# A column schedule, the rows of two weights and the first gate frames moved in a one-core encoder layer

## The chip, the core and the metric

The kernel runs on one core of one Trainium2 chip. The metric is device time in microseconds, of one launch; lower is better. All data are float32, and every product must keep almost all of that precision.

## What is computed

One layer over 2048 frames of a new stream and 32 frames of a running one, width 1024. Two mixers share one input projection; then come an output projection, a gate and an embedding product.

```python
hn = rmsnorm(h, g_mix)
proj = hn @ w_in                       # (2080, 1024) @ (1024, 3072)
hA, bA, cA, zA, vB, zB = split(proj)   # 512 columns each
u = cA * hA                            # causal width-3 convolution over frames
yA = bA * conv3(u) * silu(zA)
pooled = trailing_mean(vB, windows=(2, 4, 8, 16)) - vB
yB = (pooled @ pool_w per group) * pool_scale * silu(zB)
h = h + concat([yA, yB]) @ w_out       # 1024 x 1024
gate = sigmoid(rmsnorm(h, g_ple) @ w_ple_gate)
h = h + (p @ w_ple) * gate             # p has 256 columns
y = rmsnorm(h, g_final)
```

The last rows of u and vB are returned as states.

## The kernel before

**Products.** Each float32 operand is split by a cast on ScalarE into a rounded high part and by a subtraction on VectorE into the rest (`split`, L81 and L84; weights L197 and L198); three matmuls per block then take high x high, high x low, low x high. On top of this, two-by-two blocks of frames and weights are multiplied by a scheme of seven products in place of eight. A frame group thus needs seven pieces named 11, 21, T2, T1, T3, 22 and T4 (sums and differences of its quarters), a weight the pieces 11, 12, S2, S1, S3, S4 and 22. In the w_out and gate products frames and weights have changed sides: there the weights have the pieces T1 to T4.

**Stage 1, input projections (0 to 572 us).** Frames go in two groups of 1024 (`GROUPS`). A unit (group, j) computes 128 columns of each of the six projections, in three pairs: zb/v, c/h and za/b, in this order. Twelve matmuls of 128 x 512 per step, seven steps per pair, named x, y and z by their PSUM banks (x_zbv, y_zbv, z_zbv ...). Raw weight columns are loaded by SP as raw_zbv_0a, raw_zbv_0b and so on (L550; half a megabyte, from rows of w_in). While group 0 is computed, the pieces of group 1 are prepared: `next_columns` takes the four 128-frame columns of both halves of the group, one after the other (the fourth first, then 0, 1, 2). For a column, `frame_sums` loads two frame tiles (xt), takes their sums of squares on ScalarE (L94, kept in program order), normalizes them on VectorE (L453), transposes on TensorE (pt_g, L460, kept in program order too), forms the seven pieces and stores each on POOL's queue to DRAM (L523, p_d11, p_dT1 ...). It is a generator; `at_pace(steps, num, den)` advances it by num/den steps at every step of a unit, 24 calls per unit and 72 in the three units (0,1) to (0,3):

```python
for i, _ in enumerate(frame_sums(ahead.pop(c), f"g1_{c}", dst)):
    if i == 10 and after is not None:
        ahead[after] = columns_in(1, after, nc.gpsimd)
    yield
yield
```

So the loads of the next column's frame tiles are issued at the eleventh step, on POOL. When group 0 is done, `load_group` reads the seven pieces back in one 2 MB DMA each, on POOL (L537, tiles B). The first unit of group 1 runs its zb/v and c/h pairs in turn, and loads raw_ch into the ring `xin` (four buffers), which the staged pieces and frame tiles of the columns use too (`spare_ring`).

**Stage 2, output projection (572 to 757 us).** First the embedding products of seven frame tiles (e, L109; p @ w_ple, with pps the prepared frames of p and wp the weight), then w_out for pairs of tiles (`seven`, x_o, y_o, z_o, L185). Meanwhile the pieces of w_out are made from its upper rows wo_t 0 to 3 (`tops`) and lower rows wo_b 0 to 3 (`bots`) by `weight_parts` (L195 to L198). Frames y and residual rows x come in by SP; tiles lie in the rings xh (4 buffers), ya (5), cmb (8), qa (2) and st (4).

**Stage 3, gate (758 to 978 us).** The other nine embedding products (e_7 to e_14 and the short e_16) run with pps loads from pp_d and the weight wq from wl_d. wg_t and wg_b are the rows of the gate weight. Then follow the gate's seven products per pair of tiles (x_g, y_g, z_g). A pair's frames are made by `prep_g(i)`, two steps: `turned_here` (the odd tile, hn_1, four loads and a transpose on VectorE, L1486) and a second step with `turned` (the even tile: copies ho on ScalarE L1473, transposes pth on TensorE L1475) and the sums and splits.

The scheduler orders instructions on each engine by the program's order, the dependences and its own estimate of times; loads are issued by SP in one order, and by POOL in another, and each queue's next instruction waits for the one ahead.

Of the kernel before, what the change touches and what calls it, by code (L numbers as in the profile page):

```python
# [36 lines left out]
def trunk(ctx, tc, x_p, x_s, c_conv, c_pool, p_p, p_s, g_mix, w_in, conv_w, conv_b, pool_w,  # L37
# [320 lines left out]
    def ring4(t, name):  # L358
        return t.tile([P, D], F32, tag="t", name=name)

    def load_y(i, m, pool=None):
        a = []
        for half in range(2):
            t = ring4(pool or ya, f"y_{i}_{half}").rearrange("p (k t) -> p k t", k=KH)
            nc.sync.dma_start(t[:, :, :m], y_d[half * KH:half * KH + KH, :, i * P:i * P + m].rearrange("k p t -> p k t"))
            a.append(t)
        return a
# [7 lines left out]
    with ExitStack() as s1:  # L375
# [98 lines left out]
        def frame_sums(xs, tag, dst):  # L474

            xs = [x_stat(x, True) for x in xs]
            yield  # L480
            for x in xs:
                normal(x)
                yield
            yield
            f12, f1, f21 = (ftile(f"{c}_{tag}") for c in ("f12", "f1", "f21"))
            sub = lambda o, x, y: nc.vector.tensor_tensor(o, x, y, op=ALU.subtract)
            steps = four(xs, tag)
            p11, p12 = next(steps)
            nc.scalar.copy(f12, p12)
            sub(f1, f12, p11)  # L490
            dst("11", p11)
            yield
            dst("T1", f1)
            yield
            p21, p22 = next(steps)
            nc.scalar.copy(f21, p21)
            sub(f1, p22, f1)
            sub(f12, p22, f12)
            yield
            dst("21", p21)  # L500
            yield
            dst("22", p22)
            yield
            dst("T2", f1)
            sub(f21, f21, f1)
            yield
            dst("T3", f12)
            yield
            dst("T4", f21)
            yield  # L510
# [736 lines left out]
        for gi, tbs in enumerate(GROUPS):  # L1247
            if gi == 1:
                B = load_group(1)
            for j in range(4):  # L1250
                u = Unit(gi, tbs, j)
                if gi + j == 0:
                    u.plain()
                    B0["T4"] = piece_of(seventh("B0_T4"), 0)
                    nc.sync.dma_start(B0["T4"].bitcast(F32), p_d["T4"])
                    p_d["T4"] = tc.dram_tile([P, KH, 2, NB], F32, name="p_dT4b")
                    aside = at_pace(next_columns(3, 0, 1, 2), 3, 4)
                    continue
                if gi == 1 and j == 1:
                    aside = at_pace(chain(turn_p(), new_frames(), ple_weights()), 1, 1)  # L1260
                u.seven(B, aside, gi == 1 and j == 0)
# [3 lines left out]
    with ExitStack() as s2:  # L1265
# [88 lines left out]
        S, W = {}, {}  # L1354
        with tc.issue_after(last_raw):
            early_pps = [load_pps(qa.tile([P, 2, 2, P], F32R, tag="q", name=f"pps_{i}"), i, nc.sync) for i in range(2)]
            first_y = load_y(0, 2 * P, xh)
            tops, _ = rows_of_weight(ya, "wo_t", w_out, 0)
        weight_slot(W, "wo", *PLACES[0])
        near = weight_seventh(W, "wo")  # L1360
        for i in range(2, EARLY):
# [7 lines left out]
            loaded.append(last.ins)  # L1369

        more = prep_h(0, lower_rows)
        first_x = [load_rows(xh, "x", b, x_p) for b in range(2)]
        weight_parts(W, tops, None, "11", "T1")
        weight_slot(W, "wo", *PLACES[1])
        space = acts[0].tile([P, SLOT], F32, tag="hn", name="eouts")
# [67 lines left out]
        weight_parts(W, tops, None, "11", "T1")  # L1443
        shared = slot("wq")
        wp = [[shared[:, (2 * k + h) * D:(2 * k + h + 1) * D] for h in range(2)] for k in range(2)]
        for k in range(2):
            for h in range(2):
                nc.sync.dma_start(wp[k][h].bitcast(F32), wl_d[k][h])
        bots, _ = rows_of_weight(cmb, "wg_b", g_d, 1)

        rest_e = [*range(EARLY, NT - 2), NT - 1]

        def ring(what, i):
            if what == "pps":
                return st.tile([P, 2, 2, P], F32R, tag="t", name=f"pps_{i}")
            if what == "out" and rest_e.index(i) % 4 < 2:
                return cmb.tile([P, D], F32, tag="c", name=f"eout_{i}")
            return ring4(xh, f"e{what}_{i}")

        _, run = embed(rest_e, wp, ring, nc.gpsimd)  # L1460
        for c in range(len(rest_e)):
            run(c)


        def turned(i):

            r, n = tiles[i]
            t = load_rows(ya if i else xh, "hn", i, h_d, queue=nc.sync).rearrange("p (q k c) -> p k q c", q=4, k=KC)
            out = []
            for half in range(2):  # L1470
                pt = tbank(f"pth_{i}_{half}")
                o = qa.tile([P, KH, P], F32, tag="q", name=f"ho_{i}_{half}")
                nc.scalar.copy(o[:n].rearrange("p k (q c) -> p k q c", q=4), t[:n, half * KH:half * KH + KH])  # L1473
                for k in range(KH):
                    nc.tensor.transpose(pt[:, k * P:k * P + n], o[:n, k], ident[:n, :n])  # L1475
                out.append(pt.rearrange("p (k t) -> p k t", k=KH))
            return out
# [178 lines left out]
        def prep_g(i):  # L1656
# [18 lines left out]
            def second():  # L1675
                a21, a22 = lower
                s1 = comb("S1", a21, a22, ALU.add, whole)
                a11, a12 = turned(i)
                put("11", a11)
                s2 = comb("S2", s1, a11, ALU.subtract)  # L1680
                s3 = comb("S3", whole(a11), a21, ALU.subtract, whole)
                put("12", a12)
                put("S2", s2)
                s4 = comb("S4", a12, s2, ALU.subtract)
                put("S1", s1)
                put("S3", s3)
                put("S4", s4)
                put("22", a22, whole)
# [3 lines left out]

        S = {}
        steps = prep_g(0)
        steps[2]()
        weight_slot(W, "wg", *PLACES[1])
        weight_parts(W, tops, bots, *PLACES[1])
        W["21"] = halves(shared)[2:]
# [5 lines left out]
        W["T4"] = halves(shared)[:2]  # L1704
        for k in range(KH):
            weight_part(W, "T4", k, tops[k], bots[k], True)
        steps[3]()

        def short_gate():
            n = tiles[NT - 1][1]  # L1710
            A = short("gl", turned(NT - 1), n)
            h, e = (load_rows(*a) for a in ((xh, "h", NT - 1, h_d), (ya, "e", NT - 1, e_d)))
            yield
            plain("gl", A, W, n, *short_ops(h, e, n))
            done_g(NT - 1, h)
            yield

        short_steps = short_gate()
        for i in range(0, NT - 3, 2):
            A = S.pop(i)  # L1720
            h = [load_rows(xh, "h", i + b, h_d) for b in range(2)]
            e = [load_rows(ya, "e", i + b, e_d) for b in range(2)]
            seven(f"g{i}", A, W, *gate_ops(h, e, P, f"g{i}", i), prep_g(i + 2))
            done_g(i, h[0])
            if i in (2, 4):
                next(short_steps)
            if i + 2 < NT - 3:
                done_g(i + 1, h[1])
# [29 lines left out]
```

## Time and profile before

| | |
|---|---|
| three runs | 979.29, 979.32, 973.89 us; median 979.29 |
| profiled execution | 979.49 us |
| its span, first to last instruction | 977.7 us |
| TensorE matmul busy | 909.3 us, 93% of the span |
| VectorE busy | 697.0 us, 71% |
| ScalarE busy | 458.4 us, 47% |
| GpSimd (POOL) busy | 148.5 us, 15% |
| mean granted TensorE clock | 0.973 of full speed |

Engines are called PE (TensorE), PEld (its weight loads), DVE (VectorE), ACT (ScalarE), POOL and SP. In a row, `out<-in` are tiles by their names, without buffer numbers; `x12` is a count; what stands in brackets at a row's end is the idle time before it and what ended this. SPq is an instruction that issues a DMA on SP's queue. The profile's views cut the same execution in different ways: groups of instructions, waits, the chain of waits from the end back, the timeline of an engine, windows with the busy time of each engine, and the DMA view.

### The profile page before, as it was taken

How to read it: one execution, taken by the hardware profiler on the slowest of the kernel's cores; microseconds unless marked ns; L12 is line 12 of the kernel's file. 1: busy time of each engine (PE TensorE's matmuls, PEld its weight loads, DVE VectorE, ACT ScalarE, POOL GpSimd, SP SyncE). 2: the span in 40 equal slices, each digit the busy share in tenths (PEclk: the TensorE clock that was granted, in tenths of full speed). 3: DMA queues.
4: the chain of work that ended last, by engine and by line, in shares of the span. 5: the costliest groups of instructions: out<-in, count | busy, mean ns of one | idle time of the engine just before them, and what ended most of it. 6: DMA issues, size and time to landing. Idle time of an engine off the chain costs nothing.

```text
span 977.7 us, 12213 instructions
## 1 busy us (share of the span) xinstructions
PE 909.3 (93%) x4186; PEld 727.9 (74%) x4186; DVE 697.0 (71%) x1148; ACT 458.4 (47%) x828; POOL 148.5 (15%) x289
## 2 busy tenths in 40 slices
PE   8999999998950999999999998999999889999996
PEld 6788877887840888866678886778788668777885
DVE  6994888896920678763776759956565859689884
ACT  7643544554500444442344347444344656455553
POOL 3110031221220103110000010121211201111112
PEclk9999999999985999999999999999999899999999
DMA  8265294565599217487764285885677784546553
GB/s 267 59 194 199 82 288 151 188 209 165 170 382 375 65 46 238 144 297 239 219 196 134 94 309 220 257 255 200 214 268 255 251 294 150 191 155 238 181 194 132
DMA packets 115099, 199.57 MB, mean 204 GB/s; under 512 B 13270, under 2 KB 72062, under 8 KB 114013
## 3 DMA queue, kind: packets, MB, share of 16 engines
q1 hardware_dynamic: 93469, 127.67, 40.6%
q0 software_dynamic: 19120, 66.72, 20.0%
q10 hardware_dynamic: 2448, 4.39, 1.2%
q8 instruction: 33, 0.54, 0.2%
q14 instruction: 29, 0.24, 0.1%
HBM read 133.06 MB, written 65.67 MB: 203 GB/s over the span
## 4 chain that ended last, share of the span: by engine, by line
PE 51%; DMA 12%; DVE 8%; issue 6%; ACT 3%; POOL 1%; SPq 0%; POOLq 0%; ACTq 0%; DVEq 0%
PE x_o L185 6%; PE x_zbv L616 5%; PE x_ch L616 5%; PE x_g L185 5%; DMA raw_ch_0a<-in_w_in_dram 5%; PE x_zab L616 4%; PE z_ch L616 3%; PE z_g L185 3%; PE e L109 3%; PE z_o L185 3%; PE z_zbv L616 3%; PE z_zab L616 2%; PE y_o L185 1%; PE new L1112 1%; DMA hn<-h_d 1%
## 5 line engine op out<-in xcount | busy, mean ns | idle before, releaser
L616 PE MATMUL x_ch<-B,w_ch 128*128 128x512 f32 x84 | 22.0, 414 | 34.7 <-ACT w_ch L81 34.7
L185 PE MATMUL x_o<-wo_T,y_S 128*128 128x512 f32 x192 | 46.6, 392 | 4.0 <-ACT c_o L1285 3.4
L185 PE MATMUL z_g<-wg,g_S 128*128 128x512 f32 x192 | 47.9, 394 | 0.1
L185 PE MATMUL z_o<-wo,y_S 128*128 128x512 f32 x192 | 47.6, 390 | 0.0
L185 PE MATMUL x_g<-wg_T,g_S 128*128 128x512 f32 x192 | 46.6, 390 | 0.0
L616 PEld LDWEIGHTS x_ch<-B,w_ch 128*128 128x128 f32 x84 | 16.7, 201 | 39.2 <-ACT w_ch L81 35.1
L185 PEld LDWEIGHTS x_o<-wo_T,y_S 128*128 128x128 f32 x192 | 35.8, 188 | 12.7 <-ACT c_o L1285 4.3
L616 PE MATMUL x_zbv<-B,w_zbv_S 128*128 128x512 f32 x168 | 42.5, 403 | 3.0 <-ACT zs L936 3.0
L616 PE MATMUL x_zab<-B,w_zab_S 128*128 128x512 f32 x168 | 41.1, 393 | 0.9 <-ACT V L936 0.9
L616 PE MATMUL x_ch<-B,w_ch_S 128*128 128x512 f32 x168 | 41.8, 392 | 0.0
L185 PEld LDWEIGHTS z_o<-wo,y_S 128*128 128x128 f32 x192 | 36.0, 188 | 7.7 <-DVE y_S L84 0.3
L185 PEld LDWEIGHTS x_g<-wg_T,g_S 128*128 128x128 f32 x192 | 36.0, 188 | 7.5
L185 PEld LDWEIGHTS z_g<-wg,g_S 128*128 128x128 f32 x192 | 35.4, 188 | 7.8 <-ACT c_g L1497 0.7
L616 PE MATMUL z_zab<-B,w_zab_S 128*128 128x512 f32 x168 | 41.1, 392 | 0.0
L616 PE MATMUL z_ch<-B,w_ch_S 128*128 128x512 f32 x168 | 40.7, 391 | 0.0
L616 PE MATMUL z_zbv<-B,w_zbv_S 128*128 128x512 f32 x168 | 40.6, 391 | 0.0
L616 PEld LDWEIGHTS x_zbv<-B,w_zbv_S 128*128 128x128 f32 x168 | 32.4, 195 | 11.0 <-ACT zs L936 3.4
L616 PEld LDWEIGHTS x_zab<-B,w_zab_S 128*128 128x128 f32 x168 | 31.2, 188 | 8.5 <-ACT V L936 1.4
L616 PEld LDWEIGHTS z_zbv<-B,w_zbv_S 128*128 128x128 f32 x168 | 31.4, 188 | 7.3 <-issue 0.8
L616 PEld LDWEIGHTS x_ch<-B,w_ch_S 128*128 128x128 f32 x168 | 31.3, 188 | 7.2 <-issue 0.8
L616 PEld LDWEIGHTS z_ch<-B,w_ch_S 128*128 128x128 f32 x168 | 31.3, 188 | 7.2 <-issue 0.8
L616 PEld LDWEIGHTS z_zab<-B,w_zab_S 128*128 128x128 f32 x168 | 31.2, 188 | 7.2 <-issue 0.8
(561 smaller groups left out, 2296.1 us busy)
## 6 DMA issues: line engine op xcount, KB each, us to landing
wn<-in_w_in_dram SPq DMA_DIRECT2D x24, 512.0 KB, 5.2
p_dT<-T POOLq DMA_DIRECT2D x16, 512.0 KB, 5.8
y<-y_d SPq DMA_DIRECT2D x16, 512.0 KB, 5.8
x<-in_x_prompt_dram SPq DMA_DIRECT2D x16, 512.0 KB, 4.1
h<-h_d SPq DMA_DIRECT2D x16, 512.0 KB, 5.2
e<-e_d SPq DMA_DIRECT2D x15, 512.0 KB, 4.6
out_dram<-h POOLq DMA_DIRECT2D x14, 512.0 KB, 3.7
B<-p_d POOLq DMA_DIRECT2D x3, 2048.0 KB, 16.0
```

Of the source, the lines that this page charges most:

```text
L109: nc.tensor.matmul(ps, pps[:, a, k], wp[k][b][:, cs], start=k + q == 0, stop=k == 1 and q == 2)
L185: nc.tensor.matmul(ps[:n], lhs[:, k, a, :n], w[b][:, k], start=start and k + q == 0, stop=k == KH - 1 and q == 2, skip_group_check=True)
L616: nc.tensor.matmul(ps, lhs[:, k, x], b[:, k, y], start=start and k + q == 0, stop=stop and k == KH - 1 and q == 2, skip_group_check=True)
L1112: nc.tensor.matmul(ps[g * DEC:g * DEC + DEC, :NB // 2].rearrange("p (kind j c) -> p kind j c", kind=2, j=4), xs[:, k], t[:, g], start=k == ...
```

## The change

Three edits. (1) A column of `frame_sums` has one step less, the pace goes from 3/4 to 13/18 of a step per call, and since the load of the next column hangs on step ten, it now comes after T4's step instead of T3's. (2) The upper rows of w_out go to other rings (0 and 1 to xh, 2 and 3 to ya) and are loaded between other loads: 0 first, then the first residual rows x on POOL's queue, then 1, 2, the first frames y, half of the third frames' load, then 3. (3) Two pps and the first gate frames (hn_0, `first_h`) are loaded ahead; the embedding products run after `prep_g(0)` is set up, with its first step after the third and its second step after the fifth product; the short gate's load is a step of its own.

```diff
-    def load_y(i, m, pool=None):
-        a = []
-        for half in range(2):
-            t = ring4(pool or ya, f"y_{i}_{half}").rearrange("p (k t) -> p k t", k=KH)
+    def load_y(i, m, halves=2):
+        a = early_y if i == 2 and halves == 2 else []
+        for half in range(len(a), halves):
+            t = ring4(ya, f"y_{i}_{half}").rearrange("p (k t) -> p k t", k=KH)
...
             for x in xs:
                 normal(x)
                 yield
-            yield
...
-                    aside = at_pace(next_columns(3, 0, 1, 2), 3, 4)
+                    aside = at_pace(next_columns(3, 0, 1, 2), 13, 18)
...
-            first_y = load_y(0, 2 * P, xh)
-            tops, _ = rows_of_weight(ya, "wo_t", w_out, 0)
+            row = lambda pool, k: load_rows(pool, "wo_t", k, w_out)
+            tops = [row(xh, 0)]
+            first_x = [load_rows(xh, "x", b, x_p, queue=nc.gpsimd) for b in range(2)]
+            tops += [row(xh, 1), row(ya, 2)]
+            first_y = load_y(0, 2 * P)
+            early_y = load_y(2, 2 * P, halves=1)
+            tops.append(row(ya, 3))
...
         more = prep_h(0, lower_rows)
-        first_x = [load_rows(xh, "x", b, x_p) for b in range(2)]
...
+        got = {c: load_pps(st.tile([P, 2, 2, P], F32R, tag="t", name=f"pps_{EARLY + c}"), EARLY + c, nc.sync) for c in range(2)}
...
         bots, _ = rows_of_weight(cmb, "wg_b", g_d, 1)
+        first_h = load_rows(xh, "hn", 0, h_d)
...
-            if what == "out" and rest_e.index(i) % 4 < 2:
+            if what == "out" and rest_e.index(i) < 3:
...
-        _, run = embed(rest_e, wp, ring, nc.gpsimd)
-        for c in range(len(rest_e)):
-            run(c)
+        _, run = embed(rest_e, wp, ring, nc.gpsimd, got=got)
...
         S = {}
         steps = prep_g(0)
-        steps[2]()
+        for c in range(len(rest_e)):
+            run(c)
+            if c in (2, 4):
+                steps[2 if c == 2 else 3]()
         weight_slot(W, "wg", *PLACES[1])
...
-        steps[3]()
...
         def short_gate():
             n = tiles[NT - 1][1]
-            A = short("gl", turned(NT - 1), n)
+            t = load_rows(ya, "hn", NT - 1, h_d)
+            yield
+            A = short("gl", turned(NT - 1, t), n)
...
-            if i in (2, 4):
+            if i in (0, 2, 4):
                 next(short_steps)
```

`load_rows(pool, name, k, src, queue)` loads 128 rows into a tile of the given ring, on SP unless a queue is named.

Three places show how the orders move. First SP's queue where group 1 begins; zs_3 and c_s_3 are results of the last unit of group 0, raw_zbv_0, raw_zab_0 and raw_ch_0 the raw weights of the first unit of group 1. Before:

```order
L550 DMA raw_zbv_0b<-in_w_in_dram 128x8x128
L834 DMA y_d<-zs_3_2034 128x512
L550 DMA raw_zab_0a<-in_w_in_dram 128x8x128
L550 DMA raw_zab_0b<-in_w_in_dram 128x8x128
L550 DMA raw_ch_0a<-in_w_in_dram 128x8x128
L550 DMA raw_ch_0b<-in_w_in_dram 128x8x128
L834 DMA y_d<-c_s_3_2037 128x512 x2
```

The same place of SP's queue in the changed kernel:

```order
L549 DMA raw_zbv_0b<-in_w_in_dram 128x8x128
L833 DMA y_d<-zs_3_2038 128x512
L549 DMA raw_ch_0a<-in_w_in_dram 128x8x128
L549 DMA raw_ch_0b<-in_w_in_dram 128x8x128
L549 DMA raw_zab_0a<-in_w_in_dram 128x8x128
L549 DMA raw_zab_0b<-in_w_in_dram 128x8x128
L833 DMA y_d<-c_s_3_2041 128x512 x2
```

The raw_ch loads have passed the raw_zab loads. At the same place POOL stores the last pieces of the third column (the last three are p_dT_172 with T2, p_dT_174 with T3 and p_dT4b with T4) and reads the group back. Before:

```order
L523 DMA p_d_175<-22_1_2_2418 1024x1x128
L523 DMA p_dT_172<-T_1_2_2452 1024x1x128
L537 DMA B_0_2570<-p_d_170 128x4096
L523 DMA p_dT_174<-T_1_2_2475 1024x1x128
L523 DMA p_dT4b<-T_1_2_2496 1024x1x128
L537 DMA B_0_2570<-p_d_171 128x4096
```

And POOL's queue in the changed kernel:

```order
L522 DMA p_d_175<-22_1_2_2355 1024x1x128
L522 DMA p_dT_172<-T_1_2_2393 1024x1x128
L522 DMA p_dT_174<-T_1_2_2427 1024x1x128
L522 DMA p_dT4b<-T_1_2_2461 1024x1x128
L536 DMA B_0_2570<-p_d_170 128x4096
L536 DMA B_0_2570<-p_d_171 128x4096
```

All stores now precede the first read. Second, ScalarE in the first pair of the unit (0,3), at the last casts of the second column and the sum of squares of the third (xt_2). Before:

```order
L936 COPY zs_3_2034<-x_zbv_3_2055 128x512
L81 CAST T_1_1_2074<-f_g_1_1880 128x4x128
L81 CAST w_zbv_3_22_2183<-raw_zbv_3b 128x4x128
L81 CAST w_ch_3_11_2230<-raw_ch_3a 128x4x128
L976 ACTIVATE zs_3_2034<-zs_3_2034 128x512
L81 CAST T_1_1_2099<-f_g_1_1882 128x4x128
L94 ACTIVATE junk,ssq_x_2_2152<-xt_2_2078 128x1024
L936 COPY zs_3_2034<-x_zbv_3_2055 128x512
L81 CAST w_ch_3_12_2246<-raw_ch_3a 128x4x128
L94 ACTIVATE junk,ssq_x_2_2158<-xt_2_2080 128x1024
```

And ScalarE there in the changed kernel:

```order
L81 CAST T_1_1_2059<-f_g_1_1823 128x4x128
L81 CAST w_zbv_3_S_2104<-raw_zbv_3a 128x4x128
L81 CAST w_zbv_3_S_2132<-s_zbv_3_2048 128x4x128
L81 CAST w_zbv_3_S_2149<-raw_zbv_3b 128x4x128
L994 ACTIVATE V_2_1485<-V_2_1485 128x512
L81 CAST w_zbv_3_S_2167<-raw_zbv_3a 128x4x128
L935 COPY zs_3_2038<-x_zbv_3_2067 128x512
L81 CAST w_zbv_3_22_2184<-raw_zbv_3b 128x4x128
L81 CAST w_ch_3_11_2253<-raw_ch_3a 128x4x128
L975 ACTIVATE zs_3_2038<-zs_3_2038 128x512
L935 COPY zs_3_2038<-x_zbv_3_2067 128x512
L94 ACTIVATE junk,ssq_x_2_2120<-xt_2_2063 128x1024
```

Before, the cast of T4 (T_1_1_2099) and the sum over xt_2_2078 stand between the two copies zs_3<-x_zbv_3; now T4 (T_1_1_2059) is cast ahead of both copies and the sum follows them. Third, SP's queue at the entry of the gate stage; hn_6432 and hn_6322 are hn_1, hn_6258 is hn_0, pps_6254 and pps_6256 are pps_7 and pps_8 before, pps_6242 and pps_6244 in the changed kernel. Before:

```order
L1484 DMA hn_6432<-h_d 32x4x256
L1351 DMA wg_b_6246<-g_d 128x1024
L1484 DMA hn_6432<-h_d 32x4x256
L1351 DMA wg_b_6248<-g_d 128x1024
L1484 DMA hn_6432<-h_d 32x4x256 x2
L1351 DMA wg_b_6250<-g_d 128x1024
L1351 DMA wg_b_6252<-g_d 128x1024
L1448 DMA wq<-wl_d_61 128x1024
L1448 DMA wq<-wl_d_62 128x1024
L1448 DMA wq<-wl_d_63 128x1024
L1448 DMA wq<-wl_d_64 128x1024
L129 DMA pps_6254<-pp_d 128x512
```

And SP's queue there in the changed kernel:

```order
L1486 DMA hn_6322<-h_d 32x4x256
L1350 DMA wg_b_6250<-g_d 128x1024
L372 DMA hn_6258<-h_d 128x1024
L1350 DMA wg_b_6252<-g_d 128x1024
L1486 DMA hn_6322<-h_d 32x4x256 x2
L129 DMA pps_6242<-pp_d 128x512
L1350 DMA wg_b_6254<-g_d 128x1024
L1350 DMA wg_b_6256<-g_d 128x1024
L129 DMA pps_6244<-pp_d 128x512
L1452 DMA wq<-wl_d_61 128x1024
L1452 DMA wq<-wl_d_62 128x1024
L1452 DMA wq<-wl_d_63 128x1024
```

hn_0 and both pps have passed wq, and the fourth load of hn_1 has gone behind it (it comes after two more pps).

## Rows read from the trace of the kernel before

**Rows 1.** Waits of TensorE, whole span: us in total, times, longest us.

```profile
PE x_ch L616 <- ACT w_ch L81: 34.7, 1, 34.7
PE pth L1475 <- ACT ho L1473: 4.9, 3, 2.4
PE e L109 <- DMA pps<-pp_d: 4.0, 1, 4.0
PE x_o L185 <- ACT c_o L1285: 3.4, 2, 2.2
PE x_zbv L616 <- ACT zs L936: 3.0, 1, 3.0
PE x_o L185 <- DVE x L1280: 1.3, 1, 1.3
```

**Rows 2.** Chain that ended last, 255 to 325 us: start us, us, what.

```profile
270.35 46.85 DMA raw_ch_0a<-in_w_in_dram
317.89 4.52 PE x_ch L616 x12
322.41 2.73 PE y_zbv L616 x12
```

**Rows 3.** DMA view, 284 to 310 us: packets, MB, share of 16 engines.

```profile
q0 software_dynamic: 728, 10.62, 96.9%
q1 hardware_dynamic: 731, 0.37, 4.7%
```

**Rows 4.** DMA view, 312 to 317 us.

```profile
q1 hardware_dynamic: 2641, 1.33, 107.9%
```

**Rows 5.** Timeline of POOL, 266 to 284 us: start us, us, instruction, idle before.

```profile
266.15 0.84 POOL L523 DMA_DIRECT2D p_d<-22_1_2_2418  x1 [7.91 <-ACT T L81]
267.68 0.75 POOL L537 DMA_DIRECT2D B<-p_d  x1
282.51 0.53 POOL L537 DMA_DIRECT2D B<-p_dT  x1 [7.68 <-DMA p_dT<-T]
```

**Rows 6.** Timeline of the SP queue, 262 to 300 us.

```profile
262.41 0.33 SPq L834 DMA_DIRECT2D y_d<-zs  x1
268.32 0.38 SPq L550 DMA_DIRECT2D raw_zab_0a<-in_w_in_dram  x1
```

**Rows 7.** Timelines of TensorE, 279 to 325 and 336 to 347 us.

```profile
280.19 3.00 PE L616 MATMUL x_zbv<-B,w_zbv 128*128 128x512 f32 x12
344.02 1.30 PE L616 MATMUL x_zab<-B,w_zab 128*128 128x512 f32 x5
```

**Rows 8.** Windows: us, busy of PE, PEld, DVE, ACT, POOL, granted clock, DMA share, GB/s.

```profile
283.00:318.00 35.00, 0.31 (x2) 0.11 (x1) 0.13 (x1) 0.78 (x2) 1.09 (x3) 0.56 0.99 386
240.00:270.00 30.00, 30.00 (x141) 24.67 (x141) 29.66 (x52) 15.45 (x29) 4.90 (x6) 1.00 0.55 163
```

**Rows 9.** Timeline of VectorE at 266 us.

```profile
266.15 0.68 DVE L578 TENSOR_TENSOR raw_zab_3a<-raw_zab_3a 128x512 f32<-128x512 f32 x1
```

**Rows 10.** Timelines of ACT, TensorE and POOL, 215 to 236 us.

```profile
225.87 0.62 ACT L81 CAST T<-f_g 128x512 fp32r<-128x512 f32 x1 [4.11 <-DMA p_dT<-T]
228.78 4.61 PE L616 MATMUL x_zbv<-B,w_zbv_S 128*128 128x512 f32 x12 [2.98 <-ACT zs L936]
227.91 0.85 POOL L523 DMA_DIRECT2D p_dT4b<-T  x1 [4.88 <-DVE T L84]
```

**Rows 11.** DMA view, 218 to 222 us: issues, KB, us to landing.

```profile
xt<-in_x_prompt_dram POOLq DMA_DIRECT2D x1, 512.0 KB, 7.9
```

**Rows 12.** Timeline of TensorE, 755 to 822 us.

```profile
755.32 2.88 PE L185 MATMUL x_o<-wo_T,y 128*128 128x512 f32 x12
792.75 1.22 PE L185 MATMUL x_g<-wg,g 128*128 128x512 f32 x2
```

**Rows 13.** Windows as in rows 8, 746 to 767 us.

```profile
746.00:761.00 15.00, 12.20 (x54) 9.76 (x52) 12.33 (x20) 9.03 (x16) 1.45 (x3) 1.00 1.03 363
761.00:767.00 6.00, 4.80 (x11) 3.79 (x12) 4.37 (x9) 3.28 (x7) 2.06 (x4) 0.54 0.57 227
```

More of the change, by code (lines that the diff above doesn't have):

```diff
@@ L1455, in ring, with turned @@
                 return st.tile([P, 2, 2, P], F32R, tag="t", name=f"pps_{i}")
-            if what == "out" and rest_e.index(i) % 4 < 2:
+            if what == "out" and rest_e.index(i) < 3:
                 return cmb.tile([P, D], F32, tag="c", name=f"eout_{i}")
             return ring4(xh, f"e{what}_{i}")
-        _, run = embed(rest_e, wp, ring, nc.gpsimd)
-        for c in range(len(rest_e)):
-            run(c)
-        def turned(i):
+        _, run = embed(rest_e, wp, ring, nc.gpsimd, got=got)
+        def turned(i, t=None):
             r, n = tiles[i]
-            t = load_rows(ya if i else xh, "hn", i, h_d, queue=nc.sync).rearrange("p (q k c) -> p k q c", q=4, k=KC)
+            t = (t or load_rows(ya, "hn", i, h_d)).rearrange("p (q k c) -> p k q c", q=4, k=KC)
             out = []
@@ L1677, in second @@
                 s1 = comb("S1", a21, a22, ALU.add, whole)
-                a11, a12 = turned(i)
+                a11, a12 = turned(i, None if i else first_h)
                 put("11", a11)
```

## The prediction

> **What bounds the kernel now.** I read the waits of TensorE first, because it is busy for 93% of the span and only its gaps can give much time [rows 1]. One wait is half of all its idle time: 34.7 us before x_ch. The others of size are 3.0 (x_zbv), 3.4 and 1.3 (x_o), 4.0 (e) and 4.9 in three pieces (pth). Second, the chain of waits around the large gap [rows 2]: the frame pieces' writes end at 270.35 us, then comes the load raw_ch_0a for 46.85 us, then its cast, then x_ch at 317.89. Half a megabyte does not take 46.85 us by itself, so third comes the DMA view. Between 284 and 310 us the POOL queue passed 728 packets with 10.62 MB and the SP queue 731 packets with 0.37 MB [rows 3]. That is one packet of SP for each packet of POOL: SP's packets hold 512 bytes (0.37 MB / 731), POOL's some 15 KB (10.62 MB / 728), and SP gets 28 packets per us. Once POOL's reload of the frame pieces is through, SP passes 2641 packets in 5 us, 528 per us [rows 4]. A raw weight load is 512 KB in pieces of 512 bytes, 1024 packets: 2 us on free engines, 36 us beside the reload. So w_ch does not wait for bandwidth but for its place: the two raw_zab loads stand ahead of it on SP (the first issued at 268.32 [rows 6]), and the seven 2 MB reloads run on POOL meanwhile [rows 5].
>
> The Trainium skill ("DMA: Bandwidth & Descriptors", Queues, rings and completion order) says that each DMA engine takes turns between the queues that have work and changes over only at packet boundaries; the trace agrees, 728 against 731 packets.
>
> **Term 1, the frame columns (w_ch).** Each of the three columns loses one step, and the pace goes from 3/4 to 13/18, so 3 x 13 + 13 = 52 steps at 4/3 calls (the last at call 70 of 72) become 48 at 18/13 (call 67). By the orders, the last column's T3 and T4 writes now precede the first reload on POOL, and raw_ch_0a and 0b precede raw_zab on SP. raw_ch_0a waits for the write of 22, which before was issued at 266.15 and landed at 270.35 [rows 2, 5]; in VectorE's order that piece moves 15 places forward, some 9 us at 0.6 us each. So raw_ch_0a should issue right after y_d<-zs, 262.4 us [rows 6], with T1 and T2 landed by about 263, and both loads (4 us of packets) land near 268 to 270, ahead of the reload's first packets. B's first piece cannot come earlier: it waits for the end of TensorE's y_zab. I keep its issue at 267.7. Seven pieces at 10.62 MB per 26 us (5.1 us each) then run without the pause of 7.7 us before T3 [rows 5], and end near 307.
>
> TensorE then goes on at 280.19 + 2.72 = 282.9 with x_ch instead of 317.89 [rows 2, 7]. Its next steps use a piece every 5.4 us, which is slower than pieces arrive. Before, x_zab began at 344.02, 26.1 us after x_ch [rows 7]; 1.8 of this was x_ch at half clock (4.52 against 2.73 for twelve matmuls [rows 2]; the granted clock is 0.56 over the gap [rows 8]). At full clock x_zab is due at 282.9 + 24.3 = 307.2. But it needs raw_zab_0a, now the load beside the reload: issued at about 270.5 (its buffer is freed by w_zab_S4, now behind T4), 1024 packets at 28 per us would take until 307, and landing and a cast add 2 to 3. I take x_zab at 309.8, a new wait of 2.6 us: 344.0 - 309.8 = 34.2 us gained. Bounds: 36.8 with no wait, and 26.1 if raw_zab comes as late as raw_ch did.
>
> By that section of the Trainium skill alone, raw_zab_0a's 1024 packets outlast the reload's 7 x 128 = 896 turns by 128 packets, hardly 0.3 us at the free rate; the sum would be the same.
>
> **Term 2, what the columns cost elsewhere.** VectorE works 29.66 of the 30 us from 240 to 270 [rows 8]. In its order w_zab_S2 moves ten places back, behind T3 and T4; the op at its new place (raw_zab_3a<-raw_zab_3a) began at 266.15 before [rows 9]. S2 then ends near 267.4, while TensorE's third matmul of that step needs it at 267.0. I take -0.5 us (0 to -2). Nothing hides it, since no other engine waits less.
>
> **Term 3, the statistics of the columns.** ScalarE holds each column's sum of squares in program order. Before, the third column's stood behind a cast that waited 4.1 us for a write, and then for the x load (7.9 us [rows 11]); x_zbv waited 2.98 us and then ran 4.6 us instead of 2.9 [rows 10], 4.7 together. After, T3 and T4 are cast earlier, so the load is issued some 4 us earlier, though it now stands behind the T4 write on POOL and has one step less to arrive; and in ScalarE's order zs<-x_zbv, the copy that x_zbv waits for, now stands ahead of the sum. I take +3.5. Bounds: +4.7, and -5, the wait of POOL for such a T4 (4.88 us [rows 10]) if the first column, whose load moves from ahead of the T4 write to behind it, has no slack.
>
> **Term 4, upper output rows.** The first output products wait 3.4 + 1.3 = 4.7 us for ScalarE's and VectorE's late copies [rows 1], because weight splits and carries compete there. With wo_t 0 and 1 loaded some 20 us earlier, their casts and splits move ahead of the embedding products, and the x tiles go to POOL's queue, where only stores stand behind them. I take +3; bounds +4.7 and -2 (wo_b_3 now stands behind the first e_d store on POOL).
>
> **Term 5, gate entry.** x_o ends at 758.2 and x_g starts at 792.75, 34.55 us [rows 12]. Work in between at full clock: 96 matmuls at 2.72/12 = 21.8, eight short ones 1.8, eight transposes 1.2: 24.8. So 9.7 us are lost: 4.0 for pps and 2.4 for the transposes [rows 1], some 3.3 to the clock, which stands at 0.54 after the gap [rows 13]. After, pps_7 is there, the transposes stand amid the products, so 2.4 goes. But wq is late next. The DMA engines are full (1.03, 363 GB/s) from 746 to 761 [rows 13]. Ahead of wq's last piece the queue gains hn_0 and two pps (1 MB, 2.9 us at that rate) and loses a quarter of hn_1 (0.4); and SP now holds wg_b_1 and all behind it until the store of x_12 lands, some 2.4 us, of which I count half, since the engines have a backlog. wq's last piece came before the wait for pps ended, 762.2, less 0.7 for pps_7 itself: about 761.5, and now 761.5 + 3.7 = 765.2. The first pieces come 4 us before the last, so some ten matmuls run meanwhile; 86 more take 19.5, the clock 3, short ones and transposes 3.0: x_g at 790.7. Gain 2.0, and 1.0 of the later pth waits (4.9 - 2.4 [rows 1]), since frames are split a step earlier: +3. Bounds: -4 (wq another 6 us late) and 9.7 + 1.
>
> **Sum.** 34.2 - 0.5 + 3.5 + 3 + 3 = 43.2 us off the profiled execution of 979.5 us (span 977.7): 936. The median of the runs is 979.3, so nothing is to be scaled.
>
> **Rivals.**
> 1. *Starvation only changes its victim.* raw_zab_0a is on the same queue with the same 512-byte packets; if it is issued later than 270.5 or the reload slips, it lands like raw_ch_0a did (317.2). Then x_zab starts at 317.9 and the gain falls by 8.1: 944. For it: the 1:1 packets. Against: x_zab has 24 us of other products ahead of it.
> 2. *VectorE becomes the bound.* With ten ops more ahead of w_zab_S2 (6 us) and no idle gap used, 240 to 283 stretches by 6 us and the reload with it, and term 2 costs 6 more: 942, with a lost clock 945.
> 3. *The change does not do what it says.* If 22, T1 or T2 are still written after the reload starts, raw_ch starves as before. Only terms 3 to 5 are left: 979.5 - 9.5 = 970.
> 4. *Slower.* x loads stand behind T3 and T4 on POOL in all three columns, and the sums of squares, transposes and all later writes are pinned behind them. A load takes 7.9 us [rows 11], a T4 wait 4.9 [rows 10]; three steps of TensorE are 8.2. If T4 is not early, each column comes 4.6 us late: 13.8 us of stalls, the last column spills over the end of its unit, raw_ch starves as before (no term 1), and the reload is late by up to another 4.6. With terms 4 and 5 that is 979.5 + 18.4 - 6 = 992. It decides if the load lands over 8.2 us after T4's step. Against: T4's buffers come free earlier too.
>
> **How the numbers follow.** Forecast 0.62 (its own range 926 to 946, by the bounds of terms 1, 3, 4 and 5 added as independent), rival 1 0.18, rival 2 0.08, rival 3 0.07, rival 4 0.05. The range of 925 to 958 holds the forecast and rivals 1 and 2 with room for both at once, and leaves out 3 and 4. Measurements of this kernel tell about 1% (10 us) from no change: faster 0.92 (forecast, rivals 1 and 2, half of 3), within 1% 0.03 (the other half of 3), slower 0.05 (rival 4).
>
> **What would show it.** Right: raw_ch_0a lands before 272; no TensorE gap above 4 us between 270 and 320; a small wait of x_zab for w_zab near 307; x_zbv without its 3.0; the first e waits for wq instead of pps, and pth waits for nothing. Wrong: a gap above 8 us at x_zab (rival 1), w_zab_S waits at 266 (rival 2), raw_ch_0a landing after 300 (rival 3), waits of ScalarE's sums for xt loads in each column (rival 4).

## The result, and the profile after

The changed kernel takes 949.8 us (median of four runs, 948.0 to 951.6) against 979.3 for the kernel before beside it: a ratio of 0.971, 95% interval 0.967 to 0.975. It is faster by some 29 us; 43 were forecast, and the time lies in the range (925 to 958).

TensorE is now busy for 96% of a span of 948.3 us. The waits of TensorE after, in us, times, longest, answer to [rows 1]:

```profile
PE x_zab L615 <- ACT w_zab L81: 6.2, 1, 6.2
PE e L109 <- ACT eouts L167: 3.5, 1, 3.5
PE x_o L185 <- ACT c_o L1284: 2.9, 2, 2.2
PE e L109 <- DMA wq<-wl_d: 2.7, 3, 1.5
```

The wait of 34.7 at x_ch and that of 3.0 at x_zbv are gone. New are 6.2 at x_zab, where 2.6 were forecast, and 3.5 at e for ScalarE's copies, which the forecast did not have (its low bound for that stage, -2, stood for a late load). Where the time went shows in the starts of a few products in the two traces:

| stretch, by products of TensorE, us | before | after | gained | forecast |
|---|---|---|---|---|
| start to x_zbv of group 1 | 280.19 | 279.16 | 1.0 | 3.0 (terms 2, 3) |
| from there to x_zbv with T4 | 71.31 | 42.99 | 28.3 | 34.2 (term 1) |
| from there to the first e | 220.94 | 222.86 | -1.9 | 0 |
| first e to the end of x_o | 185.76 | 189.21 | -3.5 | 3 (term 4) |
| end of x_o to the end | 219.5 | 214.1 | 5.4 | 3 (term 5) |

The -1.9 is no part of the change: a second trace of the changed kernel (e11) has 221.04 there. The stretch behind x_o differs by some us from trace to trace (214.1 and 215.5 in the two traces of the changed kernel, 209.8 and 211.0 in e3 and e2, which have the same gate), so its term is better read from times (below).

**The large gap.** SP's queue, POOL's and TensorE's timelines after, as in [rows 5 to 7]:

```profile
261.58 0.38 SPq L549 DMA_DIRECT2D raw_ch_0a<-in_w_in_dram  x1
262.13 0.85 SPq L549 DMA_DIRECT2D raw_ch_0b<-in_w_in_dram  x1
268.93 0.37 SPq L549 DMA_DIRECT2D raw_zab_0a<-in_w_in_dram  x1
...
266.42 1.29 POOL L536 DMA_DIRECT2D B<-p_d  x2
...
279.16 2.88 PE L615 MATMUL x_zbv<-B,w_zbv 128*128 128x512 f32 x12
281.88 2.88 PE L615 MATMUL x_ch<-B,w_ch 128*128 128x512 f32 x12
312.73 2.50 PE L615 MATMUL x_zab<-B,w_zab 128*128 128x512 f32 x5 [6.21 <-ACT w_zab L81]
```

Both raw_ch loads now leave 4 us before the reload's first piece, and x_ch follows x_zbv at once, 36 us earlier than before. From there TensorE runs without a gap up to 306.5 and x_zab, which waits for its weight. ScalarE's cast of that weight waits for the load, and the DMA view tells why (269 to 272, then 272 to 308 us):

```profile
312.06 1.14 ACT L81 CAST w_zab<-raw_zab_0a 128x512 fp32r<-128x512 f32 x2 [9.84 <-DMA raw_zab_0a<-in_w_in_dram]
...
q0 software_dynamic: 201, 0.99, 106.7%
...
q0 software_dynamic: 1019, 14.39, 96.1%
q1 hardware_dynamic: 985, 0.50, 4.9%
```

SP (q1) passes nothing from 269 until 272, and then 985 packets beside POOL's 1019: 27.4 a us, one for one, as in [rows 3]. The 1024 packets of raw_zab_0a need 37.4 us from 272 at that pace, so until about 309; then come landing and cast. After the wait the clock is low. Windows, columns as in [rows 8]:

```profile
306.00:313.00 7.00, 0.79 (x4) 0.37 (x3) 0.29 (x1) 0.94 (x2) 0.65 (x1) 0.77 1.06 215
313.00:330.00 17.00, 17.00 (x68) 13.86 (x69) 10.79 (x20) 5.96 (x11) 0.00 (x0) 0.89 0.48 113
```

The granted clock is 0.77 over the wait and 0.89 behind it, a mix of 2.4 and 1.2 GHz. From x_zab to the T4 step TensorE takes 9.4 us for the same 33 matmuls for which it took 7.5 before.

### The profile page after: what moved, and what is told of

Same layout as the page of the kernel before. It is cut to its first block, busy times and chain, and to the rows that moved or that the text cites. A ratio compares the mean times of both kernels' runs of the same rounds, so it can differ in the third digit from the quotient of the medians.

```text
span 948.3 us, 12212 instructions
## 1 busy us (share of the span) xinstructions
PE 911.1 (96%) x4186; PEld 728.1 (77%) x4186; DVE 696.5 (73%) x1148; ACT 457.4 (48%) x828; POOL 150.3 (16%) x291
## 5 line engine op out<-in xcount | busy, mean ns | idle before, releaser
L615 PE MATMUL x_zbv<-B,w_zbv_S 128*128 128x512 f32 x168 | 40.6, 391 | 0.0
L1518 DVE SCALAR_TENSOR_TENSOR h<-h,rstd_f,g_bc 128x1024 f32<-128x1024 f32 (+1 forms) x15 | 19.2, 1283 | 15.4 <-POOL rstd_f L77 15.2
L81 ACT CAST y_S<-y_fS 128x512 fp32r<-128x512 f32 x28 | 17.1, 619 | 25.3 <-PE x_o L185 11.6
## 6 DMA issues: line engine op xcount, KB each, us to landing
B<-p_d POOLq DMA_DIRECT2D x3, 2048.0 KB, 16.3
```

The costliest lines, as they stand in the source:

```text
L81: ins = nc.scalar.copy(hi, src)
L615: nc.tensor.matmul(ps, lhs[:, k, x], b[:, k, y], start=start and k + q == 0, stop=stop and k == KH - 1 and q == 2, skip_group_check=True)
L1518: nc.vector.scalar_tensor_tensor(h[:n], h[:n], rf[:n], g_bc[:n], op0=ALU.mult, op1=ALU.mult)
```

## The experiments

Twelve kernels ran. Ratios are to the kernel before on the same chip (median 976 to 977 us there); a hundredth is 9.8 us.

| run | median us | ratio, 95% interval |
|---|---|---|
| changed kernel, again (e11) | 947.9 | 0.9710 (0.9687 to 0.9733) |
| e1 columns alone | 948.1 | 0.9713 (0.9687 to 0.9739) |
| e2 rows undone | 944.6 | 0.9679 (0.9656 to 0.9702) |
| e3 wo_b_3 on SP | 943.9 | 0.9675 (0.9650 to 0.9699) |
| e4 gate alone | 971.2 | 0.9953 (0.9938 to 0.9968) |
| e5 reload in quarters | 946.5 | 0.9686 (0.9671 to 0.9701) |
| e6 before, in quarters | 962.0 | 0.9852 (0.9824 to 0.9881) |
| e7 wo_b_3 on SP, pps_8 behind wq | 939.2 | 0.9628 (0.9601 to 0.9655) |
| e8 e7 and quarters | 935.4 | 0.9580 (0.9564 to 0.9596) |
| e9 e7 and x_zab later | 936.1 | 0.9590 (0.9564 to 0.9615) |
| e10 e7 and halves | 933.0 | 0.9553 (0.9522 to 0.9583) |
| e12 step alone, old pace | 972.6 | 0.9957 (0.9940 to 0.9974) |

### e1: the columns alone

The kernel before with the two edits of the frame columns (the `yield` ahead of `f12, f1, f21` removed, pace 13, 18).

> The kernel before with the frame columns' part alone (one step less in each column, pace 13/18). Theory A, read from the two traces: the columns carry nearly all of the gain. The first embedding product started 27.4 us earlier in the changed kernel (572.4 to 545.0); nothing behind it changes here, so 979.5 - 27.4 = 952 us, with the new wait of some 6 us at x_zab. Theory B, the forecast's own sizes (34.2 - 0.5 + 3.5 = 37.2): 942 us, x_zab with a wait of 2.6 or less. Rival C, that the 6 us at x_zab come from work that the other parts put there: no wait at x_zab, and 945 us.

28.0 us are gained and x_zab waits 6.1: theory A. The columns alone give as much as the whole change (28.3 by e11), and the wait of 6 us is their own.

### e2, e3: the upper output rows

e2 puts the hunks on `tops`, `first_x`, `first_y` and `load_y` back. e3 keeps them and changes one queue:

```
-                last = (nc.sync if k < KH - 1 else nc.gpsimd).dma_start(bots[0], ...)
+                last = nc.sync.dma_start(bots[0], ...)
```

> The changed kernel with the output rows' part undone (rows 0 to 3 of the upper output weights, x tiles and first y as before). Theory A: that part cost time. The wait of 3.5 us before the seventh embedding group goes and the clock behind it recovers, the waits of x_o go back from 3.7 to 4.7: 3 to 4 us faster than the changed kernel, 946 us, and from the first embedding product to x_o 19.2 us as before instead of 24.6. Rival B, the forecast: the part gains 3 us, so that without it the time is 953.

> The changed kernel with the load of wo_b_3 (the last lower row of the output weights) on SP's queue like the other three, instead of POOL's, where it stands behind the first e_d store. Theory A: VectorE's first T2 difference waits for that load and ScalarE's cast of it stands ahead of the copies that free the banks; issued 4.4 us earlier, the load lands near 556 instead of 560.5, within the banks' cover of TensorE (to 558.9): the wait of 3.5 us at e and 1.6 us of slow clock go, 945 us. Rival B: the four rows share one full queue, the last of them lands no earlier than 560, and the wait only moves to another row: 949 to 950 us, with 3 us or more at e.

Both are some 3 us faster than the changed kernel by the ratios. Their intervals just overlap with that of e11, so the traces have to tell. In the changed kernel, on POOL, VectorE, ScalarE and TensorE:

```profile
551.99 0.55 POOL L1372 DMA_DIRECT2D wo_b<-in_w_out_dram  x1 [2.50 <-issue]
...
560.54 0.69 DVE L195 TENSOR_TENSOR wo_t<-wo_b,wo_t 128x512 f32<-128x512 f32 x1 [5.88 <-DMA wo_b<-in_w_out_dram]
...
561.26 0.62 ACT L197 CAST wo_T<-wo_t 128x512 fp32r<-128x512 f32 x1 [5.95 <-DVE wo_t L195]
561.78 0.58 ACT L167 COPY eouts<-e 128x512 f32<-128x512 f32 x1
...
562.41 7.33 PE L109 MATMUL e<-wp,wo_T 128*128 128x512 f32 x24 [3.52 <-ACT eouts L167]
```

Read it from the bottom: TensorE has no free bank until ScalarE copies one out; the copy stands behind a cast, the cast waits for VectorE's difference, and that for the load of wo_b_3, issued behind an e_d store. Then 24 matmuls take 7.33 us for 5.73. But the load is not what changed. In the kernel before it goes out on POOL as well, and hardly sooner:

```profile
579.28 0.55 POOL L1368 DMA_DIRECT2D wo_b<-in_w_out_dram  x1 [4.09 <-DMA y_d<-c_s]
...
588.70 1.14 ACT L197 CAST wo_T<-wo_t 128x512 fp32r<-128x512 f32 x2 [3.37 <-DVE wo_t L195]
```

Counted from the first e (572.44 before, 545.01 in the changed kernel), the load goes out after 6.8 and 7.0 us, and the first cast of wo_T starts after 16.3 us in both. What differs is ScalarE's order. Before, and in e2, eight copies of e stand ahead of that cast; in the changed kernel it is four, and TensorE runs out of banks. With the load on SP the same stretch runs through:

```profile
548.40 13.76 PE L109 MATMUL e<-wp,wo_T 128*128 128x512 f32 x60
562.00 2.88 PE L185 MATMUL x_o<-wo,y 128*128 128x512 f32 x12
568.85 4.60 PE L185 MATMUL x_o<-wo_T,y_S 128*128 128x512 f32 x12 [2.60 <-ACT c_o L1284]
```

From the first e to x_o it is 24.6 us in the changed kernel and 19.2 in e2, in e3 and before. One step of theory A was wrong: in e3 the load goes out 6.6 us after the first e, hardly sooner than the 7.0 of the changed kernel, but lands 2 us earlier, and six copies instead of four stand ahead of the cast; e3 does not tell these two apart. And with its defect gone the edit gains nothing: x_o still waits 2.6 for c_o, as with the old order (2.9 in e1). The copy c_o stands behind the casts of T2, and T2 needs the lower rows; upper rows that come earlier only bring T1 forward.

### e4, e7: the gate's entry

e4 is the gate's part alone on the kernel before. e7 is e3 and one load of pps less ahead of wq:

```
-        got = {c: load_pps(...) for c in range(2)}
+        got = {c: load_pps(...) for c in range(1)}
```

> The kernel before with the gate's part alone (first gate frames turned and split between the embedding products, loads in the new order). Theory A, from the two traces: x_o's end to the span's end was 219.5 us before and 214.1 after, so 5.4 us gained: 974 us. Theory B, the forecast's term: 3 us, 976.5. Rival C: the gain is only there because the output rows' part changed what stands ahead of it: 979.

> The changed kernel with wo_b_3 on SP and, at the gate's entry, the load of pps_8 moved from ahead of the four wq loads to behind them. Theory A: in the changed kernel SP held the wq loads behind pps_8, whose buffer came free at 729.3, until 730.46, while the wq buffer itself was free at 725.9 with the last product of T3; the wq loads go out 4 us earlier, the three waits of e for wq (2.7 us) and about 1.5 us of slow clock behind them go: 3 to 4 us less than with wo_b_3 alone, ratio to the kernel before 0.963 to 0.965, and x_o's end to x_g 26 instead of 29.5 us. Rival B: the DMA engines are full there (busy share 0.95 to 0.98 from 725 to 738), so wq lands no earlier than before or pps_8 is now the late one: the same wait, ratio 0.9675.

By its time the gate's part is worth 4.6 us (3.1 to 6.1), between both theories. What was left of the entry in the changed kernel, on SP and TensorE:

```profile
730.02 0.32 SPq L129 DMA_DIRECT2D pps<-pp_d  x1
730.46 2.01 SPq L1452 DMA_DIRECT2D wq<-wl_d  x4
...
731.34 2.88 PE L185 MATMUL x_o<-wo_T,y 128*128 128x512 f32 x12
735.74 0.49 PE L109 MATMUL e<-wq,pps 128*128 128x512 f32 x1 [1.52 <-DMA wq<-wl_d]
```

and in e7:

```profile
721.69 1.88 SPq L1452 DMA_DIRECT2D wq<-wl_d  x4
...
726.93 2.88 PE L185 MATMUL x_o<-wo_T,y 128*128 128x512 f32 x12
731.59 0.97 PE L109 MATMUL e<-wq,pps 128*128 128x512 f32 x3 [1.10 <-DMA wq<-wl_d]
```

The wq loads had stood behind pps_8, which waits for a buffer. Moved past it, they go out 5.2 us ahead of x_o's last step, not 0.9. The waits fall from 2.7 to 1.4 us, and from x_o's end to x_g it is 26.3 us (29.5 in e3, 34.55 before). e7 is 4.6 us faster than e3 by the ratios, whose intervals touch: theory A. The cure does not hold in every execution, though. e8 and e9, which have the same edit, show 26.3 and 26.8 us there, but the trace of e10 has 29.7: wq goes out 5.2 us ahead of x_o's last step and is still waited for, 2.8 us in all. Why it landed later there stays open.

### e5, e6, e8: the reload in smaller packets

The only edit, on the changed kernel (e5), on the kernel before (e6), and on e7 (e8):

```
-                nc.gpsimd.dma_start(B[q].bitcast(F32), p_d[q])
+                for k in range(KH):
+                    nc.gpsimd.dma_start(B[q][:, k].bitcast(F32), p_d[q][:, k])
```

> The changed kernel with each 2 MB reload of a frame piece issued as four loads of 512 KB, so that its packets hold 4 KB instead of 16; bytes and order of use are the same. Theory A, the queues take turns by packet: beside 4 KB packets SP's 512-byte packets get some 90 a us instead of 28 (0.41 MB per us by 4.5 KB for a pair), raw_zab_0a's 1024 packets are through some 11 us after its issue, about 282 instead of 312; the wait of 6.2 us at x_zab goes, and 1.9 us of slow clock behind it: 8 us less than the changed kernel, 941 to 943. The two raw loads then take 2.5 us from the reload, hidden. Rival B, bandwidth: the engines are full, whoever has the turn; raw_zab_0a comes with the reload's end as before, wait of 5 us or more, 949 to 950. Rival C: the reload now ends later than it is used (4 KB packets cost more each, and each load waits for the one eight before it): the wait at x_zab is replaced by waits for B pieces, 950 or more.

> The kernel before with the same edit and nothing else: the columns stay late, raw_ch_0a stays behind two raw_zab loads on SP. Theory A, turns by packet: three loads of 1024 packets at some 90 a us are through 33 us after 268, so w_ch is there near 303 instead of 317 and the wait of 34.7 us falls to 19 to 22; the gain is 12 to 15 us less what the reload's later end takes: ratio 0.985 to 0.99. Rival B, bandwidth alone: the wait stays at 33 or more, ratio 1.00. Rival C, that the order of the loads is all that counts and w_ch comes when the reload ends: the wait stays, as by B.

> The changed kernel with all three edits: reload in quarters, wo_b_3 on SP, pps_8 behind wq. If each is worth what its theory says and they add (8 + 3 + 3.5 us off the changed kernel): 935 to 937 us, ratio 0.955 to 0.957. If rival B or C holds for the reload, it is the time of the run with the other two, ratio 0.963 to 0.968.

The DMA view, 284 to 296 us, of the changed kernel:

```profile
q0 software_dynamic: 331, 4.90, 97.0%
q1 hardware_dynamic: 331, 0.17, 4.7%
```

and of e5, with the landing of raw_zab_0b, which stands behind raw_zab_0a (KB, us from its issue at 269.75):

```profile
q0 software_dynamic: 1128, 4.10, 88.1%
q1 hardware_dynamic: 1132, 0.57, 16.1%
...
raw_zab_0b<-in_w_in_dram SPq DMA_DIRECT2D x1, 512.0 KB, 28.4
```

The turns stay one for one, so SP passes 94 packets a us instead of 28, and the second load lands near 298 instead of 318 (48.7 us after its issue in the changed kernel). TensorE no longer waits at x_zab. It waits a little for the pieces themselves:

```profile
304.06 0.96 PE L616 MATMUL x_zbv<-B,w_zbv_S 128*128 128x512 f32 x3 [0.57 <-DMA B<-p_dT]
320.55 2.88 PE L616 MATMUL x_zab<-B,w_zab 128*128 128x512 f32 x12
```

So theory A holds for the turns, and rival C for a part of the price. The gain of e5 is only 2.3 us, and its interval overlaps that of e11: the first e came 4 to 6 us earlier than in the two traces of the changed kernel, and then x_o waited 4.1 and pth 3.5 us. Without the defects of the other parts, e8 against e7, the same edit is worth 4.7 us, and these intervals are apart. The reload was priced at 8; it ends later in quarters, and in e8 that takes 2.6 us: from x_zbv to the T4 step it is 35.3 us, against 32.6 in e9 and e10, where TensorE waits for no piece.

On the kernel before the edit alone brings 14.5 us, as theory A had it. w_ch came sooner than 33 us, though: x_ch waited 10.7 us and y_ch another 4.1.

```profile
297.17 4.45 PE L617 MATMUL x_ch<-B,w_ch 128*128 128x512 f32 x12 [10.72 <-ACT w_ch L81]
```

Between 272 and 284 us SP passed 2030 packets there and POOL 886: the smaller loads wait for others to land before they are issued, and while POOL pauses SP has the engines for itself:

```profile
q0 software_dynamic: 886, 3.21, 72.3%
q1 hardware_dynamic: 2030, 1.03, 29.6%
...
279.77 0.53 POOL L538 DMA_DIRECT2D B<-p_d  x1 [2.66 <-DMA p_dT<-T]
```

In the next 12 us POOL does not pause as long, and it is one for one again: 1131 packets to 1131.

### e9, e10: order of products, and halves

In e5 and e8 the scheduler had also put x_zab behind the last products of x_zbv and x_ch, so that an early load was not the only difference. e9 does that alone, with e7's edits (`self.last` is the last product of the pair run before):

```
-                half_product(X, make("11"), B["11"], True)
+                w11 = make("11")
+                with tc.issue_after(self.last) if pin else ExitStack():
+                    half_product(X, w11, B["11"], True)
```

e10 is e8 with two loads per piece in place of four.

> The run with the reload in quarters also had TensorE's order changed: x_zab stands behind the last products of x_zbv and x_ch there, some 14 us later. This run tells the two apart: the 16 KB packets of the changed kernel, wo_b_3 on SP and pps_8 behind wq as in the run with those two, and x_zab's first product held behind x_ch's last one. Theory A, the wait is only a late load: raw_zab_0a lands near 312 as in the changed kernel (that is still so), x_zab is due near 317, so no wait of x_zab above 1 us; the other products run through, since T4's piece lands at 310.6 and is needed at 312: the 7.3 us of wait and 1.9 of slow clock of the run without this edit go, 930 to 932 us, ratio 0.953 to 0.955, faster than with quarters. Rival B: the load is only pushed to another place; the last B pieces or raw_zab_0b become the wait, 935 or more, and the packets' turns are what has to be cured.

> As the run with all three edits, but each 2 MB reload in two loads, so 8 KB packets instead of 4. Theory A, turns by packet: SP passes some 49 packets a us beside them (0.41 MB by 8.5 KB), between the 28 of 16 KB packets and the 94 that were measured beside 4 KB packets; raw_zab_0a lands near 291 and is no wait; the reload gives fewer turns away and ends 2 to 4 us earlier than in quarters (317), so TensorE's small waits for B pieces (1.9 us there and the slow steps between them) go: 933 us or less. Rival B: the number of loads outstanding, not the packet, gave SP its share: with halves (8 outstanding are 8 MB, nothing pauses) SP falls back to 28 a us, raw_zab lands at 311 and the time is 939.

> The changed kernel as it is, on the chip of the two runs above, to set the others against: 947 to 951 us, ratio 0.969 to 0.973, with the waits of 6 us at x_zab, 3.5 at e and 2.7 for wq.

ScalarE and TensorE in e9:

```profile
311.77 1.14 ACT L81 CAST w_zab<-raw_zab_0a 128x512 fp32r<-128x512 f32 x2 [10.10 <-DMA raw_zab_0a<-in_w_in_dram]
...
316.76 2.88 PE L615 MATMUL x_zab<-B,w_zab 128*128 128x512 f32 x12
323.52 0.51 PE L840 MATMUL pm<-pp,pw 128*128 128x512 f32 x1 [1.16 <-ACT pp L81]
```

The load is as late as ever, and x_zab does not feel it; ScalarE does. It stands for 10.1 us with pp, the input of the small product pm, behind the cast, and pm pays 1.8 us in two waits (1.16 and 0.65); the twelve matmuls behind take 4.50 us for 2.88. e9 gains 3.7 us over e7 by the ratios (the intervals overlap; the first e comes 3.6 us earlier in the traces), not 7 to 9: rival B, with theory A's first half. e10, DMA view 284 to 296 us and ScalarE:

```profile
q0 software_dynamic: 636, 4.58, 93.3%
q1 hardware_dynamic: 637, 0.32, 9.4%
...
303.70 0.62 ACT L81 CAST w_zab<-raw_zab_0a 128x512 fp32r<-128x512 f32 x1 [1.61 <-PE x_zbv L616]
```

53 packets a us at 8 KB, between 28 and 94: the turns hold at three sizes. The cast waits for a buffer that x_zbv frees and no longer for the load, and no B piece is waited for between 299 and 330 us. Its median is the lowest of all, 933.0 us, 4.5% below the kernel before and 1.6% below the changed one. Against e7 that is clear; against e8 and e9 the intervals overlap, so that halves are better than quarters is not shown.

### e12: the step without the pace

> The kernel before with one edit alone: each frame column loses its last step; the pace stays 3/4, so the 48 steps end at call 64 instead of 67. What is asked: whether the removed step or the slower pace makes the new waits of the transposes in the first stage (0.3 + 1.3 + 0.8 of pt_g, 1.1 of z_ch), which took back some 2 us of what the columns' statistics gained, and whether the step alone brings raw_ch forward. Theory A, the removed step: the second turn of a column comes one step sooner behind the split of the first, in a bank that is not free yet, and at 3/4 it comes sooner still: the same waits or more (3.5 to 5 us), x_zbv of the next group no earlier than 278.5, x_ch without its 34 us, 947 to 950 us, ratio 0.970 to 0.973. Rival B, the pace: at 3/4 the waits of pt_g are gone, x_zbv starts 2 us earlier than with 13/18 and the time is 945 or 946. Rival C: w_ch is late again without the slower pace, ratio 0.99 or more.

Rival C holds, and this is the most telling run: w_ch is late again, by another of its two loads. SP, POOL, VectorE and TensorE:

```profile
258.55 0.38 SPq L549 DMA_DIRECT2D raw_ch_0a<-in_w_in_dram  x1
...
260.75 4.14 SPq L833 DMA_DIRECT2D y_d<-zs  x1
265.06 0.53 SPq L549 DMA_DIRECT2D raw_ch_0b<-in_w_in_dram  x1
...
264.35 1.10 POOL L536 DMA_DIRECT2D B<-p_d  x2 [6.10 <-PE y_zab L615]
...
301.51 0.69 DVE L589 TENSOR_TENSOR s_ch<-raw_ch_0b 128x512 f32<-128x512 f32 x1 [32.00 <-DMA raw_ch_0b<-in_w_in_dram]
...
307.07 4.81 PE L615 MATMUL x_zab<-B_T,w_zab 128*128 128x512 f32 x12 [32.14 <-DVE U L938]
```

raw_ch_0a is 3 us earlier than in the changed kernel, yet raw_zbv_0b and a y_d store, whose issue takes 4.14 us, have come between it and raw_ch_0b, which leaves 0.7 us after the reload's first piece instead of 4 us before it, and takes until 301. Nor did raw_ch_0a gain by its early issue: while POOL's writes of the pieces ran (429 packets from 255 to 262 us), SP passed no packet, and its first ones went in 263 to 264. VectorE waits for raw_ch_0b in program order with a sum of the unit before behind it, and TensorE stands for 32 us. The waits of pt_g in the first stage are gone at the old pace, so the step alone does not bring them (rival B's half; the slower pace without the step was not run); that is worth 1 to 2 us there (x_zbv with T4 of the last unit of group 0 starts at 233.1 for 234.2 in e1).

## Why the prediction was right, point by point

**What bounds the kernel** was right: the wait was one for a place among packets. In e5, e6 and e10 the reload moves the same bytes in smaller packets, and SP's share follows: 94 a us beside 4 KB, 53 beside 8 KB, 28 beside 16 KB. The order of products, which changed with it, is not the cause: e9 has the new order with 16 KB packets, and there the load is as late as ever. e10 speaks against the number of loads in flight: by that rival SP would have fallen back to 28. The Trainium skill ("DMA: Bandwidth & Descriptors", Queues, rings and completion order) has the engines change queues at packet boundaries; the traces agree at all three sizes (1132 to 1128, 637 to 636, 331 to 331), if the page means by a packet what the profile counts as one.

**Term 1** (34.2, measured 28.3) had the mechanism and the place of the new wait right: x_ch at 281.88 for 282.9, raw_ch issued at 261.6 for 262.4, x_zab due at 306.5 for 307.2. Its count of steps, 52 to 48, is that of four columns, where its sentence says three. The step that was mis-sized is "about 270.5 [...] 1024 packets at 28 per us would take until 307". The load was issued sooner, at 268.93, but SP passed nothing before 272, and then 27.4 a us, until about 309: some 2 of the 2.9 us by which x_zab came after 309.8. Landing and cast, taken as 2 to 3, make the rest: x_zab starts nearly 4 us after 309. The low clock behind the wait, 1.9 us, was not priced; the forecast took the old gap's 1.8 as gained and put none beside the new one. Terms 1 to 3 together ended 8 us short.

**Terms 2 and 3** (3.0 together, measured 1.0): the 2.98 us at x_zbv went as said. What failed is that no new waits were put against them: pt_g 0.3 + 1.3 + 0.8 and z_ch 1.2 us in the first stage. By e12 those of pt_g do not come at the old pace. Nor could such a gain simply be added: x_zab waits for a load, and in the changed kernel, e1, e2, e3 and e7, whose x_zbv starts between 278.4 and 279.3, the T4 step comes at 321.6 to 323.2, and no sooner where x_zbv is sooner. VectorE did not become the bound (rival 2).

**Term 4** (+3, measured -3.5) has the wrong sign. The step "their casts and splits move ahead of the embedding products" is true of about half of the casts of 11 and T1 that counted (nine of them stood behind the first e, now four) and false of T2, which waits for the lower rows. The low bound, "-2 (wo_b_3 now stands behind the first e_d store on POOL)", has the sign and names the load that is waited for, but not the reason: the load goes out hardly later than before, 7.0 us after the first e for 6.8. What failed is that the path through ScalarE was left out. Its new order has a cast that waits for that load ahead of four copies that feed TensorE, and that was to be seen in the order. e2, with the old order and the load still on POOL, has no such wait.

**Term 5** (+3; 4.6 by e4's time): right, a little low. wq was the late load, as forecast. The low clock behind its waits (0.62 from 738 to 745 us) was in the sum; wq itself was there 4.4 us after x_o's end (738.6 and 734.2), where 7.0 were supposed (765.2 and 758.2). The sign "pth waits for nothing" did not come true: it waits 2.1 us, once.

**The rivals.** "Starvation only changes its victim" was closer than its 0.18 says: 6.2 us at x_zab lie between the forecast's 2.6 and the rival's 10.7, and in e12 it happens in full, with raw_ch_0b as the victim. Rival 3 could have come true by one SP instruction: the gain hangs on a lead of 4 us.

## What to carry to other kernels

Here a load of small packets beside a bulk load on another queue got one packet for each of the bulk's, so count its packets, not its bytes: let it leave before the bulk does, or cut the bulk into smaller packets (with e7's edits 8 KB and 4 KB were both better than 16). When such a wait is scheduled away, look for the next load of the same kind, and for how many us of lead the cure rests on. A load that moves in a schedule is judged by the instructions that wait for it in program order and by what stands behind them: here a cast that waits for a weight held the copies that give TensorE its banks.

## What was not expected of the hardware

SP's issue itself stands still while its queue is starved. These two instructions take 27.19 us in the kernel before, and 26.28 in the changed kernel, each with two raw loads ahead that are not through:

```profile
270.35 27.19 SPq L550 DMA_DIRECT2D raw_ch_0a<-in_w_in_dram  x1
...
280.08 26.28 SPq L833 DMA_DIRECT2D y_d<-c_s  x1
```

In e12 the issue of raw_zab_0b takes 28.06 us; the two c_s issues take 14.4 with halves (e10) and 4.2 with quarters (e5). So a starved queue also holds back all later loads on the same engine: raw_ch_0b went out only at 297.71 in the kernel before. And one for one is not the whole law. Beside POOL's writes of the pieces, and at the start of its reload, 512-byte packets got nothing at all: none of q1 to 201 of q0 from 269 to 272 in the changed kernel. Some 1 us of this is the usual lag: raw_zbv_0b, issued at 260.35 when little else ran, passed its first packets within 1.2 us. In e12 the first packets went over 4 us after the issue at 258.55.
